# Two-layer decoder trunk on one core: the load and first norm of the first token tile, rearranged

## The chip, the cores and the metric

One core of one Trainium2 chip runs the whole kernel. The metric is device time in microseconds (us), the median of three runs. Engines named below: PE (TensorE), DVE (VectorE), ACT (ScalarE), POOL (GpSimd), SP (SyncE, which here only issues DMAs).

## What is computed

512 tokens of width 2048 pass through two layers. Each layer is `x = x + rms_norm(mixer(rms_norm(x, norm_pre)), norm_post)`.

- Layer 0: one input projection of 7168 columns (`h @ w_in`), then eight gated linear recurrence heads (HGRN2) and eight chunked gMLP groups, a concatenation and an output projection.
- Layer 1: latent attention with 16 heads (low-rank q and kv, a shared rotary key), a SiLU gate and an output projection.

What the change touches is the very first step, `rms_norm(x, norm_pre[0])`, which is `x * rsqrt(mean(x*x) + 1e-6) * w`, on its way into the first projection. All arithmetic is float32. Each float32 operand of a projection is split into a high part (rounded to the fp32r format of PE) and a low part (the rest), and a product is three matmuls: high by high, high by low, low by high.

## The kernel before

Tokens are cut into four tiles of 128. `pre_norm(i)` (L283) treats tile i: ACT squares its four chunks of 512 columns with a running sum (L286), DVE adds the four sums (L288), POOL makes the reciprocal root (`rstd_of`, L271 and L272: a multiply-add and a power), DVE scales each chunk by it and by the weight row (L292), PE transposes the chunk in four blocks against an identity (L297), ACT casts the transposed chunk into `R` as its high part (L279) and DVE subtracts to get the low part (L280). The scaled chunks lie in `B[:, 8..11]` for even tiles and `B[:, 12..15]` for odd ones. The squares themselves are not needed; their target, a junk buffer, is `G[:, 8]` for all four tiles.

The weight row `norm_pre[0]` comes by one DMA into four partitions (0, 32, 64, 96) of `B[:, 4..7]` (L97), which two engines zero first (L96). Four shuffles on DVE (L346) then spread it to all partitions.

Weights come in pieces of 512 KB. `fetch` (L147) requests one into `raw` (three buffers), `wload` (L153) splits it: ACT casts the high part `whi` (L168), DVE subtracts for the low part `wlo` (L169); `whi` and `wlo` have four buffers each. The first projection, `ia` for head pair 0, is tile-major: for token tile 0 it runs all 16 blocks of the contraction (L209 to L211, three matmuls of 256 columns each, against pieces 0 to 3), then for tile 1, and so on. ACT copies each tile's result out (L550). So tile i's matmuls need its own 16 transposed blocks, and all four tiles need pieces 0 to 3. After `ia` the projections need all four tiles at once.

All DMAs are issued by SP, in its own order. Two kinds of order matter. In the source, `at(n, f)` (L195) holds a function back until n weight pieces have been used (`tick`, L199); without it work is traced where it stands. From the traced program the Tile framework then plans the order of the instructions of each engine at compile time, by its own estimates, earlier traced work first among what it takes to be ready. At run time each engine keeps to this order and waits at the head of its queue. So an instruction traced late can stand early where the planner took the engine to be free.

The small jobs of the start: the identity (`make_identity`, L103), three small loads into `pk` (L108 to L110), which `setup_cols` (L116) transposes and uses, and `setup_masks` (L363), which builds a mask by four POOL selects (L366, L370), a DVE cast (L372) and several memsets for the recurrence heads.

Of the kernel before, what the change touches and what calls it, by code (L numbers as in the profile page):

```python
# [14 lines left out]
AF = mybir.ActivationFunctionType  # L15
ALU = mybir.AluOpType
AX = mybir.AxisListType

P = 128
# [25 lines left out]
def trunk_kernel(ctx, tc, x, positions, norm_pre, norm_post, ev_w_in, ev_lb_logits, ev_a_onorm,  # L45
                 ev_b_ln_w, ev_b_ln_b, ev_b_ws, ev_b_bias, ev_w_out, od_w_in, od_q_norm, od_w_qb,
                 od_kv_norm, od_w_kvb, od_w_out, inv_freq, out, x1_dram):
    nc = tc.nc
# [14 lines left out]
    def tp_bank():  # L63
        return ptp.tile([P, 512], F32, name="tp", tag="tp")

    R = big.tile([P, 32, 512], F32R, name="R")
    B = big.tile([P, 16, 512], F32, name="B")
    G = big.tile([P, 9, 512], F32, name="G")
    PT2 = big.tile([P, 512], F32R, name="PT2")

    def new_w(name, dt=F32):
        return big.tile([P, 16, 512], dt, name=name, tag="W")

# [12 lines left out]
    x_t = x2.rearrange("(i p) d -> i p d", p=P)  # L86
# [3 lines left out]
    def row_bc(dst, src_row):  # L90
        nc.sync.dma_start(out=dst, in_=src_row.partition_broadcast(P))

    # ---------------------------------------------------------------- constants
    W = new_w("Wa")
    for c in range(4):
        (nc.vector if c % 2 else nc.gpsimd).memset(B[:, 4 + c, :], 0.0)  # L96
    nc.sync.dma_start(out=B[0:P:32, 4:8, :],  # L97
                      in_=norm_pre[0].partition_broadcast(4).rearrange("q (c n) -> q c n", c=4))
    for c in range(4):
        nc.sync.dma_start(out=W[:, c, :], in_=x_t[0][:, c * 512:(c + 1) * 512])  # L100

    ident = const.tile([P, P], F32, name="ident")
    make_identity(nc, ident)  # L103
    mhalf = const.tile([P, 8], F32, name="mhalf")
    nc.gpsimd.memset(mhalf, -0.5)

    pk = const.tile([18, P], F32, name="pk")
    nc.sync.dma_start(out=pk[0:16, :], in_=ev_lb_logits.rearrange("l (h p) -> (l h) p", p=P))  # L108
    nc.sync.dma_start(out=pk[16:17, :], in_=ev_a_onorm)
    nc.sync.dma_start(out=pk[17:18, :], in_=inv_freq)  # L110

    cols = const.tile([P, 18], F32, name="cols")
    lb = const.tile([P, 8], F32, name="lb")
# [14 lines left out]
        nc.vector.tensor_tensor(lb, e[:, 1], e[:, 3], ALU.mult)  # L128
        nc.vector.tensor_scalar(oml, lb, -1.0, 1.0, ALU.mult, ALU.add)

    # ---------------------------------------------------------------- weights
    def wview(w):
        return w.rearrange("(k p) c -> p k c", p=P)

# [54 lines left out]
        issue_to(n + AHEAD)  # L189
        return ready.pop(n)  # L190

    # work that is traced behind a given number of weight pieces
    clock, tasks, seq = [0], [], [0]

    def at(delay, fn):  # L195
        seq[0] += 1
        tasks.append((clock[0] + delay, seq[0], fn))
# [71 lines left out]
    def rstd_of(ss, n, ncols, name, bufs=2):  # L269
        r = sm.tile([P, ncols], F32, name=name, bufs=bufs)  # L270
        nc.gpsimd.tensor_scalar(r, ss, 1.0 / n, EPS, ALU.mult, ALU.add)  # L271
        nc.gpsimd.tensor_tensor(r, r, mhalf[:, 0:ncols], ALU.pow)  # L272
        return r
# [4 lines left out]
    def split_into(dst_hi, dst_lo, src):  # L278
        nc.scalar.copy(dst_hi, src)  # L279
        nc.vector.tensor_tensor(dst_lo, src, dst_hi.bitcast(F32), ALU.subtract)  # L280

    # ------------------------------------------------------- pre norm of one token tile
    def pre_norm(i, chunks, wbc, hbuf, junk, defer=None):  # L283
        ss = sm.tile([P, 4], F32, name="pss")
        for c in range(4):
            nc.scalar.activation(junk, chunks[c], AF.Square, accum_out=ss[:, c:c + 1])  # L286
        s1 = sm.tile([P, 1], F32, name="ps1")
        nc.vector.tensor_reduce(s1, ss, AX.X, ALU.add)  # L288
        r = rstd_of(s1, D, 1, "prs", 1)

        def scale(c):
            nc.vector.scalar_tensor_tensor(hbuf[c], chunks[c], r, wbc[c], ALU.mult, ALU.mult)  # L292

        def transpose(c):
            tp = tp_bank()
            for j in range(4):
                nc.tensor.transpose(tp[:, j * P:(j + 1) * P], hbuf[c][:, j * P:(j + 1) * P], ident)  # L297
            sl = slice(i * P, (i + 1) * P)
            tpv = tp.rearrange("p (j t) -> p j t", j=4)
            split_into(R[:, 8 * c:8 * c + 8:2, sl], R[:, 8 * c + 1:8 * c + 8:2, sl], tpv)  # L300

        def step(c):
            scale(c)
            transpose(c)

        for c in range(4):
            if defer is None:
                step(c)
            else:
                at(defer + c // 2, lambda c=c: step(c))  # L310

    # ================================================================ layer 0
    ew, ow = wview(ev_w_in[0]), wview(od_w_in[0])
    qv, kvv = wview(od_w_qb[0]), wview(od_w_kvb[0])
    cuts_q = ((0, 128), (128, 192))
# [25 lines left out]
        pl["kv", p] = plan_chunk(kvv, p * 512, 512, 4, 2)  # L341
    plan_out("oo", od_w_out[0])

    wpre = [B[:, 4 + c, :] for c in range(4)]
    for c in range(4):
        nc.vector.stream_shuffle(wpre[c], wpre[c], [0] * 32)  # L346
    for i in range(NT):
        if i > 0:
            for c in range(4):
                nc.sync.dma_start(out=W[:, 4 * i + c, :], in_=x_t[i][:, c * 512:(c + 1) * 512])  # L350
            if i == 1:
                issue_to(3)
        else:
            for q in range(2):
                fetch(q)
        pre_norm(i, [W[:, 4 * i + c, :] for c in range(4)], wpre,
                 [B[:, 8 + 4 * (i % 2) + c, :] for c in range(4)], G[:, 8, :])

    mask = const.tile([P, P], U8, name="mask")
    r8 = const.tile([P, 4, 32], F32, name="r8")  # L360
# [2 lines left out]
    def setup_masks():  # L363
        mf = G[:, 7, 0:P]
        nc.gpsimd.memset(mf, 1.0)
        nc.gpsimd.affine_select(mf, mf, pattern=[[1, P]], compare_op=ALU.is_ge, fill=0.0,  # L366
                                base=0, channel_multiplier=-1)
        for b in range(1, 4):
            blk = mf[:, b * 32:(b + 1) * 32]
            nc.gpsimd.affine_select(blk, blk, pattern=[[0, 32]], compare_op=ALU.is_ge, fill=0.0,  # L370
                                    base=-32 * b, channel_multiplier=1)
        nc.vector.tensor_copy(mask, mf)  # L372
        nc.vector.memset(r8, 0.0)
        nc.vector.memset(r8[:, 0, 0::8], 1.0)
        nc.vector.memset(r8[:, 1, 7::8], 1.0)
        nc.vector.memset(r8[:, 2, 0::4], 1.0)
        nc.vector.memset(r8[:, 3, 3::4], 1.0)
        nc.vector.memset(pw, 1.0)
        nc.gpsimd.memset(G[:, 8, :], 0.0)

    setup_masks()
    S_sb = new_hs("S_sb", F32)
    nc.gpsimd.memset(S_sb, 0.0)

    cosT = const.tile([P, T], F32, name="cosT")
    sinT = const.tile([P, T], F32, name="sinT")
# [20 lines left out]
        nc.scalar.activation(sinT, r, AF.Sin, scale=sgn[:, 0:1])  # L407
        nc.scalar.activation(cosT, n, AF.Sin, scale=-1.0, bias=sgn[:, 1:2])

    # ------------------------------------------------------- HGRN2 of one head  # L410
    def t4(a):
        return a.rearrange("p (b t) -> p b t", b=4)

    def hgrn_vec(h):
        par = h % 2
        f, sg, q = W[:, par, :], W[:, 2 + par, :], W[:, 4 + par, :]
        A, kdg, KK1, kD = W[:, 8, :], W[:, 9, :], W[:, 10, :], W[:, 11, :]
        k128, q128 = W[:, 12, :], W[:, 13, :]
# [151 lines left out]
        hgrn_head(2 * p + 1, 5)  # L570
        proj_feat(pl["ga", p], r_act, ga_evac)

    # ------------------------------------------------------- gMLP, two groups at a time
    for p in range(4):
        vg = W[:, 0:2, :].rearrange("p g (i c) -> p g i c", i=4)
        lnw = B[:, 14, :].rearrange("p (w c) -> p w c", w=2)
# [57 lines left out]
        proj_feat(pl["ub", p], r_act, ub_evac)  # L634
        proj_feat(pl["gb", p], r_act, gb_evac)

    # ------------------------------------------------------- output projection, post norm, residual
    def out_proj(Wy, name, wpost_row, resid_t, junk, finish, early=KD, hook=None):
        def split_cat(k0, k1):
            for k in range(k0, k1):  # L640
# [56 lines left out]

    out_proj(W, "eo", norm_post[0], x_t, G[:, 8, :], finish0)

    # ================================================================ layer 1  # L700
    row_bc(B[:, 0, :], od_q_norm[0])
    row_bc(B[:, 1, :], od_kv_norm[0])
    C = low_rank_act()
# [39 lines left out]
        nc.gpsimd.tensor_tensor(sw[0:n], sw[0:n], sinT[0:n], ALU.mult)  # L743
        nc.vector.tensor_tensor(dst[0:n], dst[0:n], sw[0:n], ALU.add)

    # shared rotary key
    kps = mm_bank()
    stk, _ = piece(pl["kpe"])
    for k in range(KD):
# [14 lines left out]

    low_rank("ckv", B[:, 1, :], [G[:, 4 + i, :] for i in range(4)], 8, False)

    # gate path
    for c in range(8):
        def gate_evac(m, ps, c=c):
            g = B[:, 2 * c + m, :]  # L770
# [189 lines left out]
```

## Time and profile before

| what | value |
|---|---|
| median of three runs | 1623.61 us (1623.47 to 1623.64) |
| profiled execution, span on the core | 1621.9 us |
| median less span (what lies around the span) | 1.7 us |
| PE busy in the span | 1588.8 us (98%) |
| DVE, ACT, POOL busy | 760.4, 536.8, 100.8 us |
| first PE instruction | 11.05 us after the span's start |

No time of the profiled execution is given apart from its span, so its own time is taken as the span and the 1.7 us around it. The page shows PE busy from the second fortieth of the span to the last; a fortieth is 40.5 us. A busy PE is not a PE at its peak: 128x256 matmuls that start 0.12 us apart are shown with 0.28 us each.

### The profile page before, as it was taken

To read this page: it belongs to the slowest core of one execution; us is meant where nothing else is said; L and a number is where in the kernel's file an instruction comes from. 1 tells how busy PE (TensorE), PEld (TensorE's weight loads), DVE (VectorE), ACT (ScalarE), POOL (GpSimd) and SP (SyncE) were. 2 spreads that over 40 slices of the span, in tenths; PEclk is the share of its full clock that TensorE was granted. 3 is DMA by queue.
4 is the path that set the end of the run, shared out by engine and by line. 5 is a ranking of instruction groups with operands and counts; after the bars stand their busy time and mean duration, and the time that the engine had idled before them with its cause. 6 is when DMAs were issued, how large, how long until landed. Compare 5 with 4: busy or idle time off the path is not lost.

```text
span 1621.9 us, 22372 instructions
## 1 busy us (share of the span) xinstructions
PE 1588.8 (98%) x9185; PEld 1397.2 (86%) x9185; DVE 760.4 (47%) x1351; ACT 536.8 (33%) x938; POOL 100.8 (6%) x163
## 2 busy tenths in 40 slices
PE   6999999999999999999999999999999999999997
PEld 5889898898989898888899999888888888888887
DVE  7653544535534343453226543232266667663234
ACT  6322222222222212232225432222255565552221
POOL 1000000000120120200001000000000000000000
PEclk9999999999999999999999999999999999999999
DMA  6422322323233333343336423333221121232324
GB/s 205 121 85 79 92 88 77 94 81 96 89 117 98 101 85 111 115 136 100 105 97 189 137 65 92 104 92 100 85 66 56 59 59 58 93 104 92 104 91 156
DMA packets 133394, 161.14 MB, mean 99 GB/s; under 512 B 7958, under 2 KB 104744, under 8 KB 133288
## 3 DMA queue, kind: packets, MB, share of 16 engines
q1 hardware_dynamic: 133292, 159.71, 32.1%
q8 instruction: 72, 1.18, 0.3%
q14 instruction: 30, 0.25, 0.1%
HBM read 151.30 MB, written 8.39 MB: 98 GB/s over the span
## 4 chain that ended last, share of the span: by engine, by line
PE 90%; DVE 5%; ACT 2%; POOL 1%; issue 1%; DMA 1%; DVEq 0%; POOLq 0%; SPq 0%; ACTq 0%
PE mm L214 14%; PE mm L216 14%; PE mm L215 14%; PE mm L211 13%; PE mm L210 13%; PE mm L209 13%; DVE R L280 2%; PE sc L485 1%; PE sc L890 1%; DVE wlo L169 1%; DVE sc L864 1%; ACT G L868 1%; PE tp L297 1%; PE sc L891 1%; DVE R L820 1%
## 5 line engine op out<-in xcount | busy, mean ns | idle before, releaser
L169 DVE TENSOR_TENSOR wlo<-raw,whi 128x1024 fp32r<-128x1024 f32 x240 | 300.1, 1251 | 614.5 <-ACT whi L168 597.6
L168 ACT CAST whi<-raw 128x1024 fp32r<-128x1024 f32 x240 | 252.2, 1052 | 767.7 <-PE mm L215 353.0
L209 PE MATMUL mm<-whi,R 128*128 128x256 f32 (+1 forms) x1408 | 442.0, 314 | 0.1
L210 PE MATMUL mm<-wlo,R 128*128 128x256 f32 (+1 forms) x1408 | 440.6, 313 | 1.2 <-DVE wlo L169 1.2
L211 PE MATMUL mm<-whi,R 128*128 128x256 f32 (+1 forms) x1408 | 440.5, 313 | 0.0
L214 PE MATMUL mm<-R,whi 128*128 128x512 f32 x896 | 351.4, 392 | 0.0
L216 PE MATMUL mm<-R,wlo 128*128 128x512 f32 x896 | 348.9, 389 | 0.0
L215 PE MATMUL mm<-R,whi 128*128 128x512 f32 x896 | 348.8, 389 | 0.0
L210 PEld LDWEIGHTS mm<-wlo,R 128*128 128x128 f32 x1408 | 268.8, 191 | 16.8 <-DVE wlo L169 1.7
L209 PEld LDWEIGHTS mm<-whi,R 128*128 128x128 f32 x1408 | 268.8, 191 | 15.4 <-ACT whi L168 0.3
L211 PEld LDWEIGHTS mm<-whi,R 128*128 128x128 f32 x1408 | 268.8, 191 | 15.0
L216 PEld LDWEIGHTS mm<-R,wlo 128*128 128x128 f32 x896 | 168.2, 188 | 35.2
L214 PEld LDWEIGHTS mm<-R,whi 128*128 128x128 f32 x896 | 168.3, 188 | 34.5
L215 PEld LDWEIGHTS mm<-R,whi 128*128 128x128 f32 x896 | 168.3, 188 | 34.2
L214 PE MATMUL mm<-Wc,whi 128*128 128x512 f32 x160 | 62.8, 393 | 0.0
L215 PE MATMUL mm<-Wc,whi 128*128 128x512 f32 x160 | 62.7, 392 | 0.0
L216 PE MATMUL mm<-Wc,wlo 128*128 128x512 f32 x160 | 62.5, 390 | 0.0
L280 DVE TENSOR_TENSOR R<-mm,R 128x512 fp32r<-128x512 f32 x48 | 33.1, 689 | 31.3 <-ACT R L279 31.1
L280 DVE TENSOR_TENSOR R<-tp,R 128x512 fp32r<-128x512 f32 x64 | 42.7, 686 | 2.5 <-ACT R L279 1.9
L279 ACT CAST R<-tp 128x512 fp32r<-128x512 f32 x64 | 36.1, 592 | 17.6 <-PE tp L297 16.5
L279 ACT CAST R<-mm 128x512 fp32r<-128x512 f32 x48 | 28.1, 586 | 38.0 <-PE mm L216 19.5
L868 ACT ACTIVATE G<-sc,nm 128x512 f32<-128x512 f32 (+2 forms) x48 | 26.1, 545 | 35.2 <-DVE nm L867 35.1
(237 smaller groups left out, 1552.7 us busy)
## 6 DMA issues: line engine op xcount, KB each, us to landing
raw<-in_ev_w_in_dram SPq DMA_DIRECT2D x112, 512.0 KB, 3.6
raw<-in_od_w_in_dram SPq DMA_DIRECT2D x49, 512.0 KB, 3.9
raw<-in_ev_w_out_dram SPq DMA_DIRECT2D x32, 512.0 KB, 3.6
raw<-in_od_w_out_dram SPq DMA_DIRECT2D x32, 512.0 KB, 3.6
raw<-in_od_w_kvb_dram SPq DMA_DIRECT2D x16, 512.0 KB, 3.7
raw<-in_od_w_qb_dram SPq DMA_DIRECT2D x16, 384.0 KB, 3.3
Wa<-in_x_dram SPq DMA_DIRECT2D x16, 256.0 KB, 5.6
G<-in_x_dram SPq DMA_DIRECT2D x16, 256.0 KB, 4.8
```

The costliest lines, as they stand in the source:

```text
L168: nc.scalar.copy(hi[:, 0:n], raw[:, 0:n])
L169: nc.vector.tensor_tensor(lo[:, 0:n], raw[:, 0:n], hi[:, 0:n].bitcast(F32), ALU.subtract)
L209: nc.tensor.matmul(o, hh[:, sl], wh, start=first, stop=False, skip_group_check=True)
L210: nc.tensor.matmul(o, hh[:, sl], wl, start=False, stop=False, skip_group_check=True)
L211: nc.tensor.matmul(o, hl[:, sl], wh, start=False, stop=last, skip_group_check=True)
L214: nc.tensor.matmul(ps, hi, hh, start=first, stop=False)
L215: nc.tensor.matmul(ps, hi, hl, start=False, stop=False)
L216: nc.tensor.matmul(ps, lo, hh, start=False, stop=last)
L279: nc.scalar.copy(dst_hi, src)
L280: nc.vector.tensor_tensor(dst_lo, src, dst_hi.bitcast(F32), ALU.subtract)
L297: nc.tensor.transpose(tp[:, j * P:(j + 1) * P], hbuf[c][:, j * P:(j + 1) * P], ident)
L868: nc.scalar.activation(pv[j], sp[j], AF.Exp, bias=nm[:, j:j + 1], scale=C_SCALE, accum_out=su[:, j:j + 1])
```

## The change

Seven edits:

1. The four chunks of token tile 0 are requested first of all, chunks 0 and 2 on SP, chunks 1 and 3 on ACT's queue. Before, SP issued all four, and the request for the norm row stood between them.
2. For tile 0, DVE squares chunks 1 and 3 (`tensor_tensor_reduce` into `G[:, 5]`), ACT chunks 0 and 2.
3. For tile 1, the junk target of the squares is `B[:, 11]`, which holds the scaled chunk 3 of tile 0 until it has been transposed.
4. The three small loads into `pk` are issued after all loads of x.
5. `setup_masks` and the memset of `S_sb` are held back by one weight piece.
6. 24 transposes of the identity by itself run on PE, traced ahead of the shuffles; nothing reads their results.
7. Comment lines go.

```diff
     W = new_w("Wa")
+    for c in range(4):
+        (nc.sync if c % 2 == 0 else nc.scalar).dma_start(out=W[:, c, :], in_=x_t[0][:, c * 512:(c + 1) * 512])
     for c in range(4):
         (nc.vector if c % 2 else nc.gpsimd).memset(B[:, 4 + c, :], 0.0)
     nc.sync.dma_start(out=B[0:P:32, 4:8, :],
                       in_=norm_pre[0].partition_broadcast(4).rearrange("q (c n) -> q c n", c=4))
-    for c in range(4):
-        nc.sync.dma_start(out=W[:, c, :], in_=x_t[0][:, c * 512:(c + 1) * 512])
-
     ident = const.tile([P, P], F32, name="ident")
...
-    nc.sync.dma_start(out=pk[0:16, :], in_=ev_lb_logits.rearrange("l (h p) -> (l h) p", p=P))
-    nc.sync.dma_start(out=pk[16:17, :], in_=ev_a_onorm)
-    nc.sync.dma_start(out=pk[17:18, :], in_=inv_freq)
...
+    def pre_norm(i, chunks, wbc, hbuf, junk, defer=None, junk2=None):
         ss = sm.tile([P, 4], F32, name="pss")
         for c in range(4):
-            nc.scalar.activation(junk, chunks[c], AF.Square, accum_out=ss[:, c:c + 1])
+            if junk2 is not None and c % 2:
+                nc.vector.tensor_tensor_reduce(out=junk2, in0=chunks[c], in1=chunks[c], scale=1.0, scalar=0.0,
+                                               op0=ALU.mult, op1=ALU.add, accum_out=ss[:, c:c + 1])
+            else:
+                nc.scalar.activation(junk, chunks[c], AF.Square, accum_out=ss[:, c:c + 1])
...
+    for _ in range(3):
+        warm = tp_bank()
+        for j in range(8):
+            nc.tensor.transpose(warm[:, (j % 4) * P:(j % 4 + 1) * P], ident, ident)
     wpre = [B[:, 4 + c, :] for c in range(4)]
...
-                 [B[:, 8 + 4 * (i % 2) + c, :] for c in range(4)], G[:, 8, :])
+                 [B[:, 8 + 4 * (i % 2) + c, :] for c in range(4)], B[:, 11, :] if i == 1 else G[:, 8, :],
+                 junk2=G[:, 5, :] if i == 0 else None)
+
+    nc.sync.dma_start(out=pk[0:16, :], in_=ev_lb_logits.rearrange("l (h p) -> (l h) p", p=P))
+    nc.sync.dma_start(out=pk[16:17, :], in_=ev_a_onorm)
+    nc.sync.dma_start(out=pk[17:18, :], in_=inv_freq)
...
-    setup_masks()
+    at(1, setup_masks)
     S_sb = new_hs("S_sb", F32)
-    nc.gpsimd.memset(S_sb, 0.0)
+    at(1, lambda: nc.gpsimd.memset(S_sb, 0.0))
```

## Rows read from the trace of the kernel before

**Rows 1.** The line of the page that gives each engine's busy time, share of the span and count of instructions.

```profile
PE 1588.8 (98%) x9185; PEld 1397.2 (86%) x9185; DVE 760.4 (47%) x1351; ACT 536.8 (33%) x938; POOL 100.8 (6%) x163
```

**Rows 2.** Busy time by stretch: from and to in us, length, busy us of each engine with the count of its instructions, PE clock granted, share and rate (GB/s) of DMA.

```profile
0.00:50.00 50.00, 35.75 (x260) 33.52 (x261) 38.42 (x81) 30.96 (x63) 7.42 (x25) 1.00 0.57 179
50.00:400.00 350.00, 350.00 (x2009) 306.22 (x2008) 169.18 (x244) 93.86 (x140) 20.94 (x40) 1.00 0.29 90
...
37.85:50.50 12.65, 12.65 (x100) 12.27 (x101) 10.83 (x24) 7.12 (x11) 0.44 (x1) 1.00 0.27 73
20.39:41.11 20.72, 18.41 (x149) 17.36 (x149) 18.61 (x31) 13.27 (x32) 2.02 (x5) 1.00 0.48 158
```

**Rows 3.** The chain that ended last, five of its pieces in the first 16 us: start, length, what.

```profile
2.08 3.90 DMA B<-in_norm_pre_dram
6.13 2.62 DVE B L346 x4
9.13 0.55 POOL G L370 x3
...
14.17 0.58 PE mm L210
14.77 1.12 PE tp L297 x4
```

**Rows 4.** SP's queue in order of time: start, length over which the merged requests were issued, line, target and source, count.

```profile
0.79 0.86 SPq L100 DMA_DIRECT2D Wa<-in_x_dram  x2
2.08 0.66 SPq L97 DMA_DIRECT2D B<-in_norm_pre_dram  x1
2.80 0.86 SPq L100 DMA_DIRECT2D Wa<-in_x_dram  x2
...
4.80 0.95 SPq L150 DMA_DIRECT2D raw<-in_ev_w_in_dram  x2
```

**Rows 5.** Busy time by stretch, columns as in rows 2: two stretches while the first loads are under way.

```profile
2.00:4.00 2.00, 0.00 (x0) 0.00 (x0) 0.70 (x11) 0.08 (x2) 1.55 (x4) 1.00 0.86 243
4.00:6.00 2.00, 0.00 (x0) 0.00 (x0) 0.00 (x0) 1.43 (x4) 0.00 (x0) 1.00 0.76 188
```

**Rows 6.** Instructions of DVE, ACT and POOL for token tile 0 in order of time: start, length, engine, line, what, shape; in brackets the idle time before it and what ended it.

```profile
2.41 0.35 DVE L404 MEMSET sgn<- 32x1 f32 x4
...
3.99 0.63 ACT L286 ACTIVATE G<-Wa 128x512 f32<-128x512 f32 x1 [1.92 <-DMA Wa<-in_x_dram]
...
7.00 0.63 ACT L286 ACTIVATE G<-Wa 128x512 f32<-128x512 f32 x1 [1.50 <-DMA Wa<-in_x_dram]
...
8.63 0.14 DVE L288 TENSOR_REDUCE ps<-pss 128x1 f32<-128x4 f32 x1
8.87 0.19 POOL L271 TENSOR_SCALAR prs<-ps 128x1 f32<-128x1 f32 x1 [5.28 <-DVE ps L288]
...
10.24 2.74 DVE L292 SCALAR_TENSOR_TENSOR B<-Wa,prs,B 128x512 f32<-128x512 f32 x4 [0.30 <-POOL prs L272]
```

**Rows 7.** The same instruction (`tensor_tensor_reduce`) where layer 1 uses it, by line and shape: count, busy us, mean ns of one, idle before.

```profile
L864 DVE CUSTOM_DVE_ANT_0 sc<-sc,G 128x512 f32<-128x512 f32 x16 | 11.0, 690 | 0.0
```

**Rows 8.** PE in order of time, columns as in rows 6: four rows of tile 0 and one of tile 2; and the busy time of the stretch just behind PE's last instruction, columns as in rows 2.

```profile
11.05 1.97 PE L297 MATMUL tp<-ident,B 128*128 128x128 f32 x8 [11.05 <-DVE B L292]
...
16.11 1.05 PE L297 MATMUL tp<-ident,B 128*128 128x128 f32 x4
...
17.82 0.41 PE L211 MATMUL mm<-whi,R 128*128 128x256 f32 x1
...
18.19 0.28 PE L210 MATMUL mm<-wlo,R 128*128 128x256 f32 x1
...
30.74 0.60 PE L297 MATMUL tp<-ident,B 128*128 128x128 f32 x4
...
1614.00:1616.00 2.00, 0.00 (x0) 0.00 (x0) 0.89 (x3) 0.13 (x2) 0.74 (x2) 0.89 0.81 310
```

**Rows 9.** ACT, DVE, POOL and PE (PEld is its weight load) around token tile 1 in order of time, columns as in rows 6, and the first reader of `pk`.

```profile
17.21 0.59 ACT L279 CAST R<-tp 128x512 fp32r<-128x512 f32 x1
17.69 0.63 ACT L286 ACTIVATE G<-Wa 128x512 f32<-128x512 f32 x1
18.44 0.63 ACT L286 ACTIVATE G<-Wa 128x512 f32<-128x512 f32 x1
19.07 1.98 ACT L168 CAST whi<-raw 128x1024 fp32r<-128x1024 f32 x2
19.20 0.16 DVE L288 TENSOR_REDUCE ps<-pss 128x1 f32<-128x4 f32 x1 [0.68 <-ACT G L286]
19.52 0.19 POOL L271 TENSOR_SCALAR prs<-ps 128x1 f32<-128x1 f32 x1 [9.32 <-DVE ps L288]
20.16 0.19 PEld L209 LDWEIGHTS mm<-whi,R 128*128 128x128 f32 x1 [0.33 <-ACT whi L168]
20.39 0.75 DVE L292 SCALAR_TENSOR_TENSOR B<-Wa,prs,B 128x512 f32<-128x512 f32 x1 [1.03 <-POOL prs L272]
21.06 1.22 DVE L169 TENSOR_TENSOR wlo<-raw,whi 128x1024 fp32r<-128x1024 f32 x1
22.33 0.39 PE L210 MATMUL mm<-wlo,R 128*128 128x256 f32 x1 [0.41 <-DVE wlo L169]
39.93 0.23 PE L118 MATMUL tp<-ident,pk 18*128 18x18 f32 x1
```

More of the change, by code (lines that the diff above doesn't have):

```diff
@@ L280, in split_into @@
         nc.vector.tensor_tensor(dst_lo, src, dst_hi.bitcast(F32), ALU.subtract)
-    def pre_norm(i, chunks, wbc, hbuf, junk, defer=None):
+    def pre_norm(i, chunks, wbc, hbuf, junk, defer=None, junk2=None):
         ss = sm.tile([P, 4], F32, name="pss")
         for c in range(4):
-            nc.scalar.activation(junk, chunks[c], AF.Square, accum_out=ss[:, c:c + 1])
+            if junk2 is not None and c % 2:
[3 more added lines that the diff above has]
+                nc.scalar.activation(junk, chunks[c], AF.Square, accum_out=ss[:, c:c + 1])
         s1 = sm.tile([P, 1], F32, name="ps1")
```

## The prediction

> **What bounds the kernel now.** I read the page's line of engines first. PE is busy 98% of the span [rows 1], so the reader should ask only where PE is not busy or not at its pace. Busy time by stretch answers it: in the first 50 us PE is busy for 35.75, in the next 350 for all 350 [rows 2]. The change lies wholly in those first 50 us. There I read the chain of waits, then each engine in order of time.
>
> To 10.24 us the chain runs over the norm row: its DMA (requested at 2.08, landed 3.9 us later), four shuffles on DVE (6.13, 2.62 us together), then POOL, where three mask selects (0.55 us) stand ahead of the power [rows 3]. Beside it runs a second path just as long: the four chunks of x, the last two of which ACT got at 7.00 and after [rows 6]; the sum on DVE starts at 8.63, when shuffles and squares are both over. The first scale starts at 10.24 and PE's first transpose at 11.05 [rows 6, 8].
>
> From there to about 20 us four engines wait for each other in turn. From 20.39 to 41.11 DVE is the limit: 18.61 of 20.72 us busy, by scales, splits and the low parts of two weight pieces. Then PE has work in hand: 12.65 of 12.65 us from 37.85 to 50.50 [rows 2]. So a gain counts if it brings forward tile 1's first scale at 20.39, takes work out of DVE's stretch behind it, or fills PE's waits.
>
> The sum is made against the profiled execution: a span of 1621.9 us with 1.7 around it, 1623.6 in all, which is the median shown.
>
> **The change part by part.**
>
> *First scale of tile 0.* SP's two requests of chunks took 0.86 us and so do ACT's two, before anything else it has to do; ACT got its first chunk at 3.99 after 1.92 us idle [rows 4, 6], which hides the 0.86. Chunks 2 and 3 are asked for some 1.6 us earlier (about 1.2 in place of 2.80). But the norm row, which cannot be asked for before the memsets are over (2.08), now stands behind chunk 2 as well, while the DMA engines were already 86% and 76% busy [rows 4, 5]. At 243 GB/s half a megabyte is 2.1 us, so the row lands 0 to 2.1 us later. Two squares come to DVE at 0.69 each [rows 7]; they cost nothing if done before the row is in. Best case: row at 6.1, sum taken ahead of the shuffles, scale right behind them at 8.75, that is 1.5 earlier. Worst: shuffles end at 10.85, and sum, POOL and the rest of the way (8.63 to 10.24, 1.61) come behind them: 12.5, 2.2 later. Nothing in the rows is near either end, so I take the middle, +0.3.
>
> *Mask work.* From POOL's first step to the scale it is 1.37 us for tile 0 (8.87 to 10.24) and 0.87 for tile 1 (19.52 to 20.39) [rows 6, 9]; the selects are the difference, 0.5. But a memset due only at the twelfth weight piece (L404) ran at 2.41 [rows 6]: the planner fills idle engines early whatever the trace order, so the selects may stay. 0 to -0.5; I take the middle, -0.25. The DVE memsets that are held back too stood in idle time before 3 us, and none is needed within 50 us.
>
> *Warm-up.* 24 transposes at 1.97/8 = 0.25 us [rows 8] are 5.9 us on an idle PE; the identity is ready at about 2.4, so they end by 8.4, ahead of the first real one even at 8.75 plus 0.8. The granted clock is listed as 1.00 there [rows 2], yet transposes of tile 0 take 1.05 to 1.12 us in fours against 0.60 later, and matmuls 0.41 up to 17.82 against 0.28 from 18.19 [rows 3, 8]: PE ran at the lower level (1.2 GHz) until about 18 and at 2.4 GHz then. Between the first scale and the end of tile 0's transposes (17.16) the chain holds one matmul (0.58 against 0.28) and two such fours: 0.30 + 0.52 + 0.45 = 1.3 us. If PE enters at the upper level, 1.3 is saved; if not, 0. Against it: in the stretch from 1614 to 1616, where PE has no instruction left, the grant averages 0.89, so it falls there [rows 8]; and the warm-up would stop 1 us or more (up to 4.9 with the late first scale) before the real work. I take half, -0.65. The page "TensorE: Matmul & The Clock Gate" of the Trainium skill says (Part 4: PE-mode transpose) that transposes do not count as PE activity for the clock as matmuls do. By that rule this term is 0 and the sum below 0.65 higher; no row decides it, since transposes and matmuls are mixed in the low stretch.
>
> *Tile 1's squares.* With the junk in `B[:, 11]` all four wait until PE has transposed tile 0's last chunk (17.16 before); two of them used to run ahead of that. Behind each wait in ACT's queue stand the squares of tile 2 and any cast planned later. Before, the sum followed 2.04 us after 17.16 (19.20). Now it needs a cast (0.48, 17.21 to 17.69) and four squares at 0.75 (17.69 to 18.44): 3.6 with the hand-over [rows 9], 1.5 later. Lower end 0, if the squares no longer break up the casts; upper end is the rival below. I take +1.5.
>
> *What fills that wait.* The casts of pieces 2 and 3 stood behind the squares (19.07 to 21.05), and their low parts (1.2 each, 21.06 and later) in DVE's limiting stretch [rows 9]. With ACT waiting, the planner can move them ahead: 0 to -2.4. Piece 3 is asked for late (its buffer waits for piece 0), so I take one piece, -1.2. PE's own waits for piece 2 (0.33 at 20.16 and 0.41 at 22.33) then go: -0.75.
>
> *No cost.* The three `pk` loads leave SP's queue ahead of the weights (at 4.80) and pass twelve loads of x; their reader runs at 39.93 [rows 4, 9], far behind. Weight requests move up, at most to 2.74 where the norm row's request ends, but DMA is nearly full and DVE's scales end at 12.98, so the first low part could not start sooner. If the plan put that reader ahead of the loads' landing, PE would stall with all it holds behind it.
>
> Sum: +0.3 - 0.25 - 0.65 + 1.5 - 1.2 - 0.75 = -1.05. Prediction 1622.6.
>
> **Rivals.**
>
> *The start opens fully.* Row early (-1.5), clock up (-1.3), squares as above (+1.5), both pieces ahead (-2.4), PE's waits gone (-0.75): -4.4 or 1619.2. For it: each end is possible by the rows. Against: it needs the norm row to pass 1 MB of x.
>
> *Slower: ACT stands behind piece 3.* The planner puts the cast of piece 3 ahead of tile 1's squares, since it is traced earlier, and on the chip ACT waits for that load with the squares behind it. Before, the second cast ran to 21.05. Then squares 3.0 and sum to scale 1.19 (19.20 to 20.39) bring tile 1's first scale to 25.2 in place of 20.39; less two low parts already done, 2.4, that is +2.4: 1626.0. It decides from a cast that starts at 17.6 or later (17.6 + 1.0 + 3.0 + 1.2 - 2.4 = 20.4). For it: the trace order. Against: piece 0 is split earlier, so piece 3 may be there.
>
> *The warm-up does nothing and the selects stay.* The clock is low until tile 0's matmuls have run, whatever ran before: 0.65 and 0.25 drop out of the sum: 1623.5. The Trainium skill's rule on transposes, named above, would give this.
>
> **How the numbers follow.** The forecast 0.45 (its own range 1621.2 to 1624.0), the open start 0.22, the slower case 0.18, no effect of the warm-up 0.15. All low ends together give -1.5 - 0.5 - 1.3 - 2.4 - 0.75 = -6.4 with the squares at 0; all high ends 2.2 + 2.4 = +4.6; one in ten at each side is left out: 1618.7 to 1625.9. This kernel's measurement tells 0.2%, 3.25 us, from no change. Faster than that (under 1620.4) is most of the open start and a little of the forecast, 0.24; slower (over 1626.9) is the slower case with a late first scale on top, 0.08; 0.68 lies within.
>
> **What would show it.** First scale between 8.75 and 12.5: the norm row's landing and the place of the sum among the shuffles tell which. Transposes of tile 0 at 0.6 us a four: the warm-up held; at 1.05: it did not. Squares of tile 1 all behind tile 0's last transposes, and the casts of pieces 2 and 3 before or behind them. DVE's last split of tile 3 (41.1 before) and the end of `ia` (about 50.5 before) should move by about -1. The prediction is wrong if PE's later stretch moves: a new wait behind 50 us, or a plan that shifted there.

## The result, and the profile after

| | us |
|---|---|
| before, median of 20 runs | 1623.62 (1623.24 to 1624.03) |
| after, median of 20 runs | 1626.58 (1625.72 to 1627.39) |
| ratio | 1.0017, 95% interval [1.0011, 1.0023] |
| span of the profiled execution, before and after | 1621.9, 1624.3 |

The change makes the kernel 3.0 us slower. 1622.6 was predicted, with a range up to 1625.9. The 3.0 us are below the 0.2% (3.25 us) up to which the prediction speaks of no change, but they are clear of noise (the interval leaves out 1), outside the range and on the other side of the forecast.

The same views as ahead of the prediction, of the kernel after. In its file L286 and L283 are the squares on ACT and DVE, L288 the sum, L267 and L268 the root on POOL, L292 the scale, L297 the transposes, L275 and L276 the high and low part of a transposed chunk, L164 and L165 those of a weight piece, L351 the shuffles, L376 and L380 the selects, L382 the mask cast, L348 the warm-up, L560 the copy of `ia`. The page's line of engines, to be held against [rows 1]:

```profile
PE 1593.1 (98%) x9209; PEld 1401.4 (86%) x9209; DVE 761.5 (47%) x1355; ACT 535.0 (33%) x934; POOL 100.6 (6%) x163
```

PE has 24 instructions and 4.3 us more, which is the warm-up. Busy time by stretch, columns as in [rows 2]:

```profile
8.00:10.00 2.00, 0.00 (x0) 0.00 (x0) 2.00 (x7) 1.05 (x2) 1.98 (x5) 0.70 1.04 354
10.00:18.00 8.00, 4.96 (x20) 4.18 (x21) 7.90 (x12) 3.85 (x5) 0.24 (x2) 0.50 0.81 270
24.85:43.86 19.01, 16.04 (x126) 14.70 (x127) 16.24 (x29) 10.14 (x24) 2.04 (x5) 1.00 0.29 84
...
50.00:400.00 350.00, 350.00 (x2017) 306.65 (x2016) 169.74 (x244) 96.29 (x142) 20.88 (x40) 1.00 0.29 90
```

Behind 50 us nothing changed: PE is busy for all 350 us, as before, and its last matmul starts at 1615.85 in place of 1613.28, 2.57 later, about as much as at the end of `ia` (below). The loss was made in the first 50. The third row is DVE's limiting stretch, from tile 1's first scale to tile 3's last split (the low part of a transposed chunk): 19.01 us in place of 20.72 [rows 2], but begun at 24.85 in place of 20.39. The first two show the clock: granted at 0.70 in the mean from 8 to 10 us, at 0.50 (the lower level, 1.2 GHz) to 18.

Token tile 0 in order of time, DVE and POOL, columns as in [rows 6]:

```profile
4.73 0.69 DVE L283 CUSTOM_DVE_ANT_0 G<-Wa 128x512 f32<-128x512 f32 x1 [1.86 <-DMA Wa<-in_x_dram]
6.71 0.69 DVE L283 CUSTOM_DVE_ANT_0 G<-Wa 128x512 f32<-128x512 f32 x1 [1.28 <-DMA Wa<-in_x_dram]
7.51 0.16 DVE L288 TENSOR_REDUCE ps<-pss 128x1 f32<-128x4 f32 x1
7.66 0.73 DVE L351 STREAM_SHUFFLE B<-B 128x512 f32<-128x512 f32 x1
8.02 0.29 POOL L376 TENSOR_SCALAR_AFFINE_SELECT G<-G 128x128 f32<-128x128 f32 x1
8.28 0.55 POOL L268 TENSOR_TENSOR prs<-prs,mhalf 128x1 f32<-128x1 f32 x1
10.19 2.72 DVE L292 SCALAR_TENSOR_TENSOR B<-Wa,prs,B 128x512 f32<-128x512 f32 x4
```

The sum is 1.1 us earlier than in [rows 6] and the root is ready at 8.8, but the first scale moved from 10.24 to 10.19 only: the four shuffles now stand behind DVE's two squares and end at 10.2. The first shuffle (7.66) shows no wait for the norm row, so the row was there by then.

PE in order of time, to be held against [rows 8]:

```profile
2.49 4.24 PE L348 MATMUL tp<-ident 128*128 128x128 f32 x24 [2.49 <-POOL ident masks.py:199]
11.07 1.94 PE L297 MATMUL tp<-ident,B 128*128 128x128 f32 x8 [4.34 <-DVE B L292]
...
15.98 1.12 PE L297 MATMUL tp<-ident,B 128*128 128x128 f32 x4 [1.29 <-DVE R L276]
...
17.32 1.06 PE L297 MATMUL tp<-ident,B 128*128 128x128 f32 x4
```

The warm-up ended at 6.73, not near 8.4 as predicted: the 24 took 4.24 us, 0.18 each. 4.34 us of idle time lie between it and the first real transposes, and these take what they took before: 1.94, 1.12, 1.06. New is the wait of 1.29 for a low part on DVE: tile 0's last transposes end at 18.38 in place of 17.16.

DVE, ACT and POOL around token tile 1, to be held against [rows 9]:

```profile
12.83 2.35 DVE L165 TENSOR_TENSOR wlo<-raw,whi 128x1024 fp32r<-128x1024 f32 x2
15.23 1.28 DVE L276 TENSOR_TENSOR R<-tp,R 128x512 fp32r<-128x512 f32 x2
14.18 1.05 ACT L164 CAST whi<-raw 128x1024 fp32r<-128x1024 f32 x1 [0.55 <-DMA raw<-in_ev_w_in_dram]
...
18.41 0.59 ACT L275 CAST R<-tp 128x512 fp32r<-128x512 f32 x1 [0.69 <-PE tp L297]
18.89 0.64 ACT L286 ACTIVATE B<-Wa 128x512 f32<-128x512 f32 x1
19.52 1.03 ACT L164 CAST whi<-raw 128x1024 fp32r<-128x1024 f32 x1
20.45 0.63 ACT L286 ACTIVATE B<-Wa 128x512 f32<-128x512 f32 x1
21.08 0.62 ACT L286 ACTIVATE G<-Wa 128x512 f32<-128x512 f32 x1
21.69 0.62 ACT L286 ACTIVATE B<-Wa 128x512 f32<-128x512 f32 x1
22.31 0.62 ACT L286 ACTIVATE G<-Wa 128x512 f32<-128x512 f32 x1
22.92 0.62 ACT L286 ACTIVATE B<-Wa 128x512 f32<-128x512 f32 x1
23.66 0.16 DVE L288 TENSOR_REDUCE ps<-pss 128x1 f32<-128x4 f32 x1 [1.85 <-ACT B L286]
24.85 2.74 DVE L292 SCALAR_TENSOR_TENSOR B<-Wa,prs,B 128x512 f32<-128x512 f32 x4 [1.04 <-POOL prs L268]
...
43.17 0.69 DVE L276 TENSOR_TENSOR R<-tp,R 128x512 fp32r<-128x512 f32 x1 [0.58 <-ACT R L275]
53.31 0.35 ACT L560 COPY G<-mm 128x256 f32<-128x256 f32 x1
```

The target tells the squares apart: `B` is tile 1, `G` is tile 2. Tile 1's four squares begin at 18.89, once their junk target is free (18.38) and tile 0's last cast is done, and are spread to 23.54, with the cast of piece 3 and two squares of tile 2 in between. The sum comes at 23.66 (19.20 before), the first scale at 24.85 (+4.46). The shorter stretch behind it gives 1.71 back: DVE's last split is at 43.17 (40.42 before), the last copy of `ia` at 53.31 (50.70), the span 2.4 longer.

### The profile page after: what moved, and what is told of

Read it like the earlier page. It is cut to its first block, busy times and chain, and to the rows that moved or that the text cites. A ratio compares the mean times of both kernels' runs of the same rounds, so it can differ in the third digit from the quotient of the medians.

```text
span 1624.3 us, 22413 instructions
## 1 busy us (share of the span) xinstructions
PE 1593.1 (98%) x9209; PEld 1401.4 (86%) x9209; DVE 761.5 (47%) x1355; ACT 535.0 (33%) x934; POOL 100.6 (6%) x163
## 4 chain that ended last, share of the span: by engine, by line
PE 90%; DVE 5%; ACT 2%; issue 1%; POOL 1%; DMA 0%; DVEq 0%; ACTq 0%; POOLq 0%
PE mm L210 14%; PE mm L212 14%; PE mm L211 14%; PE mm L205 13%; PE mm L207 13%; PE mm L206 13%; DVE R L276 2%; PE sc L495 1%; PE sc L900 1%; PE tp L297 1%; DVE sc L874 1%; ACT G L878 1%; DVE wlo L165 1%; PE sc L901 1%; DVE R L830 1%
## 5 line engine op out<-in xcount | busy, mean ns | idle before, releaser
L165 DVE TENSOR_TENSOR wlo<-raw,whi 128x1024 fp32r<-128x1024 f32 x240 | 299.9, 1250 | 615.0 <-ACT whi L164 594.7
L164 ACT CAST whi<-raw 128x1024 fp32r<-128x1024 f32 x240 | 252.1, 1051 | 768.1 <-PE mm L211 355.6
L276 DVE TENSOR_TENSOR R<-mm,R 128x512 fp32r<-128x512 f32 x48 | 33.1, 689 | 31.4 <-ACT R L275 31.2
L276 DVE TENSOR_TENSOR R<-tp,R 128x512 fp32r<-128x512 f32 x64 | 42.6, 685 | 2.6 <-ACT R L275 2.1
L275 ACT CAST R<-tp 128x512 fp32r<-128x512 f32 x64 | 36.1, 592 | 21.5 <-PE tp L297 20.4
L275 ACT CAST R<-mm 128x512 fp32r<-128x512 f32 x48 | 28.1, 586 | 38.1 <-PE mm L212 19.5
```

Of the source, the lines that this page charges most:

```text
L164: nc.scalar.copy(hi[:, 0:n], raw[:, 0:n])
L165: nc.vector.tensor_tensor(lo[:, 0:n], raw[:, 0:n], hi[:, 0:n].bitcast(F32), ALU.subtract)
```

## The experiments

Each run was timed beside the kernel before on the same chip; "against before" is the difference of the two medians. The interval of each ratio reaches some 1.5 us to each side, so smaller differences are read from the traces. Three rows of each trace serve as a yardstick: the first scale of tile 1, DVE's last split of tile 3 and the last copy of `ia`. But a trace is one execution. Tile 0's first scale, ahead of which edit 3 changes nothing and edit 6 only adds work on an idle PE, starts at 10.24 (before), 9.63 (3 alone) and 10.46 (6 alone), so under 0.8 us a row counts only against an earlier row of its own trace. The span scatters too: from PE's last matmul to its end the traces take 8.1 to 9.2 us.

| edits present | against before | first scale, tile 1 | last split | last copy of `ia` | span |
|---|---|---|---|---|---|
| none | 0 | 20.39 | 40.42 | 50.70 | 1621.9 |
| all | +3.0 | 24.85 | 43.17 | 53.31 | 1624.3 |
| all but 3 | -1.4 | 16.44 | 38.38 | 49.12 | 1620.3 |
| 3 alone | +0.5 | 22.62 | 41.72 | 51.98 | 1622.9 |
| all but 6 | +1.9 | 24.19 | 42.33 | 52.60 | 1623.5 |
| 6 alone | +0.4 | 22.44 | 40.47 | 50.74 | 1622.6 |
| all but 3 and 6 | -1.0 | 21.30 | 40.16 | 50.18 | 1621.1 |

### Edit 3, the junk target

Undone in the kernel after:

```diff
-                 [B[:, 8 + 4 * (i % 2) + c, :] for c in range(4)], B[:, 11, :] if i == 1 else G[:, 8, :],
+                 [B[:, 8 + 4 * (i % 2) + c, :] for c in range(4)], G[:, 8, :],
```

> The changed kernel with edit 3 undone: tile 1's squares go to G[:, 8] again. Theory (hold): the 3.0 us lost come from tile 1's squares, which the junk in B[:, 11] holds behind tile 0's last transposes, so that tile 1's first scale starts at 24.85 instead of 20.39; without it the scale starts at 21 or before and the time falls by 2 to 3 us, to 1623.6 to 1624.6. Rival (order on DVE): the loss is tile 0's own, because two low parts of weights and the mask cast (2.4 us) stand ahead of its first low part on DVE; then undoing edit 3 gives back under 1 us, 1625.6 or more. A third way: the freed squares are planned ahead of tile 0's casts on ACT and hold those up until tile 1's chunks land; then tile 0's last transposes end later than 18.4 us.

Measured: 1622.02 against 1623.40 before, ratio 0.9992 [0.9983, 1.0001]. DVE and ACT around tile 1:

```profile
10.93 0.62 ACT L286 ACTIVATE G<-Wa 128x512 f32<-128x512 f32 x1
15.04 0.14 DVE L288 TENSOR_REDUCE ps<-pss 128x1 f32<-128x4 f32 x1
16.44 0.73 DVE L292 SCALAR_TENSOR_TENSOR B<-Wa,prs,B 128x512 f32<-128x512 f32 x1
```

Without the hold the planner puts tile 1's squares into ACT's idle time from 10.93 on, ahead of tile 0's first cast. In the medians the change gains 1.4 without this edit; the edit takes 4.3.

Put alone into the kernel before (same line, the other way):

> The kernel before with edit 3 alone: only the junk target of tile 1's squares is moved to B[:, 11]. Theory (hold): tile 1's squares all run behind tile 0's last transposes, its first scale moves from 20.39 to 22.5 to 23.5 us, one low part leaves the stretch behind it, and the time rises by 1 to 2 us to 1624.6 to 1625.6. Rival (order on DVE): no change beyond 0.5 us, 1623.6.

Measured: 1623.92 against 1623.40, ratio 1.0003 [0.9995, 1.0012]. There the squares start at 17.10, and three of them stand in one piece. So the edit's price is no constant: in the old order 0.5 in the medians, inside the interval (1.3 at the last copy of `ia` in the trace, which is that of the slowest of the eleven executions), in the new one 4.3.

Is it the hold, or only the other buffer? Tile 1's squares write into a piece of the same buffer that nothing holds:

```diff
-                 ..., B[:, 11, :] if i == 1 else G[:, 8, :],
+                 ..., B[:, 15, :] if i == 1 else G[:, 8, :],
```

> The changed kernel, where the junk target of tile 1 is another piece of the same buffer, the one that nothing holds at that time (tile 1's own fourth scaled chunk), so the squares are moved out of the common junk buffer but held by nothing. Theory: edit 3 costs what it costs because of the hold alone, so this equals the run with edit 3 undone: 1622.0, tile 1's four squares from 10.9 on, tile 1's first scale at 16.4. Rival: moving the target out of the common junk buffer costs something by itself (that buffer also carries the mask build and a memset on POOL): between 1622.0 and 1626.6.

Measured: 1622.13 against 1623.68, ratio 0.9992 [0.9983, 1.0001]: the time and the order of the run with edit 3 undone. It is the hold.

And tile 2's squares in between? They get the same held target, so the planner has no reason to take them first:

```diff
-                 ..., B[:, 11, :] if i == 1 else G[:, 8, :],
+                 ..., B[:, 11, :] if i in (1, 2) else G[:, 8, :],
```

> The changed kernel with tile 2's squares on the same held junk target as tile 1's, so that the planner no longer mixes them in between tile 1's: one square of tile 1, piece 3's cast, then the other three squares of tile 1 in one piece. Theory: of the 4.5 us by which tile 1's first scale is late, the squares of tile 2 in between account for about 1.3 (two of 0.63), the cast of piece 3 for 1.0 and the hold itself for the rest: sum near 22.4, first scale near 23.6, time 1625.4. Rival: the mixing costs nothing, since tile 2's squares have to be done anyway and DVE waits for them next: 1626.6.

Measured: 1625.38 against 1623.68, +1.7 in place of +3.0. DVE at tile 1:

```profile
22.45 0.16 DVE L288 TENSOR_REDUCE ps<-pss 128x1 f32<-128x4 f32 x1 [0.91 <-ACT B L286]
23.64 2.74 DVE L292 SCALAR_TENSOR_TENSOR B<-Wa,prs,B 128x512 f32<-128x512 f32 x4 [1.03 <-POOL prs L268]
```

The sum is 1.21 earlier, and so is the first scale. Of this 0.27 was there before: the first square starts at 18.62 in place of 18.89. From it to the sum are 3.83 us in place of 4.77, 0.94 less; the two squares of tile 2 had taken 1.22, but tile 1's now start 0.75 apart where they follow each other, not 0.62. The medians differ by 1.3.

### Edit 6, the warm-up

Taken out of the kernel after (the four lines of the 24 transposes):

> The changed kernel without the 24 transposes of the identity. If the warm-up has no effect on the clock of tile 0's work (the clock rose during it and fell again before 11 us), the time of the instructions of tile 0 is the same, 1.05 to 1.12 us for four transposes, and the total stays within 0.5 us of 1626.6, but for what a different plan brings. If the warm-up matters, the total rises by 1 us or more. Order on DVE: with the first low part of tile 0 planned ahead of the weights' low parts, tile 0's last transposes end 1 us earlier than 18.4 and the total falls by up to 1 us.

Measured: 1625.26 against 1623.40, ratio 1.0012 [1.0003, 1.0020]; 1.1 less than with it in the medians, 0.7 to 0.8 in the traces from the last copy of `ia` on. DVE and PE at tile 0:

```profile
12.73 0.67 DVE L276 TENSOR_TENSOR R<-tp,R 128x512 fp32r<-128x512 f32 x1
...
16.04 1.06 PE L297 MATMUL tp<-ident,B 128*128 128x128 f32 x4
```

Fours of transposes take 1.12 and 1.06 as before, so the warm-up had brought no clock. What goes is an order: without the 24 transposes tile 0's first low part (12.73) stands ahead of the weight's, presumably because the planner takes PE to be free earlier; the last transposes end at 17.10 in place of 18.38. Only half of that reaches tile 1's first scale (24.19 in place of 24.85), because three squares of tile 2 now stand among tile 1's, not two.

Alone, in the kernel before:

> The kernel before with edit 6 alone (24 identity transposes). Theory: the clock falls again between the end of the warm-up (near 6.7 us) and the first real transposes (near 11), so nothing is gained; the planner counts the warm-up as PE time and puts both low parts of pieces 0 and 1 ahead of tile 0's first low part, which costs about 1.2 us of PE wait: 1624.8, fours of transposes still 1.05 to 1.12 us. Rival: the clock that the warm-up raises is worth something even so (one of the two fours of transposes at 0.6): 1622.5 to 1623.6.

Measured: 1624.10 against 1623.75, ratio 1.0002 [0.9993, 1.001]. Both the lost order (PE waits 1.16 us for tile 0's low part at 16.12) and the fours at 1.11 and 1.05 are there, but not its price of 1.2: 0.4 in the medians, 0.04 at the last copy of `ia`. Tile 1's first scale is 2.05 later, but one weight low part (20.12) stands ahead of it that stood behind it before, and DVE's last split is at 40.47 (40.42 before).

Longer, 56 transposes (`range(3)` to `range(7)`), so that it reaches up to the real ones:

> The changed kernel with 56 instead of 24 transposes of the identity, so that PE works until just ahead of the first real transposes at 11.07 us. If only the idle gap from 6.73 to 11.07 undid the warm-up, the granted clock stays at the upper level, tile 0's fours of transposes take 0.6 us, and its last transposes end about 1 us earlier than 18.4; the total falls by 0.5 to 1.5 us to 1625.1 to 1626.1. If transposes cannot hold the clock, the fours stay at 1.05 and the total at 1626.6. If tile 1's hold hides it, the fours are short and the total falls by less than 0.5.

Measured: 1629.89 against 1623.40, ratio 1.0040 [1.0027, 1.0053]. The transposes of the warm-up by source line, in the kernel after and in this run (count, duration in ns min/median/max, first and last start in us):

```profile
L348 PE MATMUL tp<-ident x24: 272/420/476, 2.5 to 6.5; 128*128 128x128 f32 x24
```

```profile
L348 PE MATMUL tp<-ident x56: 272/273/473, 2.5 to 10.7; 128*128 128x128 f32 x56
```

PE in order of time behind it:

```profile
10.93 1.29 PE L297 MATMUL tp<-ident,B 128*128 128x128 f32 x8
...
19.64 0.58 PE L205 MATMUL mm<-whi,R 128*128 128x256 f32 x1 [7.42 <-ACT R L275]
```

Both ends of the mechanism are here. The clock rose during the warm-up (from 0.47 us a transpose to 0.27) and held: eight real transposes take 1.29 in place of 1.94. And the planner, with still more PE time ahead, put the casts of pieces 2 and 3 ahead of tile 0's first casts; ACT waited for piece 3's load, and PE 7.42 us for ACT. In that wait the clock fell: the fours behind it take 1.12 and 1.06 again.

The clock without that side effect: edit 3 undone, and the 24 transposes take x's fourth chunk as input, so they start when it lands. At the start the order on DVE and ACT is that of the run with edit 3 undone:

```diff
-            nc.tensor.transpose(warm[:, (j % 4) * P:(j % 4 + 1) * P], ident, ident)
+            nc.tensor.transpose(warm[:, (j % 4) * P:(j % 4 + 1) * P], W[:, 3, (j % 4) * P:(j % 4 + 1) * P], ident)
```

> The changed kernel with edit 3 undone, and the 24 warm-up transposes take blocks of x's fourth chunk as input in place of the identity, so that they cannot start before that chunk has landed (6.3 to 6.7 us) and end near 10.8, just ahead of the first real transposes near 11. The order on DVE, ACT and PE at the start is that of the run with edit 3 alone undone (1622.0). Theory: the clock is then still at its upper level when the real work begins; eight transposes take 1.3 in place of 1.9, fours 0.6 in place of 1.1, and tile 0's last transposes end about 1 us earlier: 1621.0. Rival: the gain is swallowed by the casts on ACT and low parts on DVE, which set PE's pace there: 1622.0, though the transposes are faster. Third: the warm-up runs past 11 and pushes the real ones: 1622.5 or more.

Measured: 1622.01 against 1623.75, ratio 0.9989 [0.998, 0.9998]. PE in order of time, and the last copy of `ia`:

```profile
6.62 5.07 PE L348 MATMUL tp<-ident,Wa 128*128 128x128 f32 x24 [6.62 <-DMA Wa<-in_x_dram]
11.53 1.04 PE L297 MATMUL tp<-ident,B 128*128 128x128 f32 x8
...
16.00 0.66 PE L297 MATMUL tp<-ident,B 128*128 128x128 f32 x4 [1.20 <-DVE R L276]
...
47.90 0.35 ACT L560 COPY G<-mm 128x256 f32<-128x256 f32 x1
```

In this trace the clock held through to tile 1, although the warm-up ran 0.5 too long. Against the run with edit 3 undone the last copy of `ia` is 1.22 earlier, and the kernel's last group of scales is still 1.20 earlier (DVE, 1612.82 in place of 1614.02); the span is only 0.5 shorter because 0.7 more passes behind them, in the part that scatters. The trace is not typical: it lists a mean granted clock of 0.999, three other executions 0.998, and seven 0.996 or 0.997, which no execution of the kernel before has (0.998 or 0.999); in those seven the clock must have fallen for a while. The medians of the two runs (-1.7 and -1.4 against before) cannot be told apart.

With 16 transposes in place of 24:

> The run with the late warm-up (24 transposes of x's fourth chunk, edit 3 undone), with 16 transposes in place of 24. In that run the warm-up ended at 11.5 and pushed tile 0's first transposes from 11.0 to 11.5. Theory: 16 end near 10.3, the real ones start at 11.0 with the clock still at its upper level, and the whole start is 0.5 us earlier: 1621.5. Rival: the idle time between 10.3 and 11.0, or that between tile 0's first eight transposes and the first matmul, now lets the clock fall, fours of transposes take 1.1 again: 1622.0 to 1622.5. The shorter warm-up also lets the planner put tile 0's first two casts on ACT ahead of tile 1's fourth square, which should bring PE's first matmul from 14.3 to about 13.5.

Measured: 1623.20 against 1623.43, ratio 1.0 [0.9991, 1.0009]: the rival, and worse than it. PE and one stretch:

```profile
10.95 1.29 PE L297 MATMUL tp<-ident,B 128*128 128x128 f32 x8 [0.97 <-DVE B L292]
...
15.72 1.11 PE L297 MATMUL tp<-ident,B 128*128 128x128 f32 x4 [1.14 <-DVE R L276]
```

```profile
12.00:14.00 2.00, 0.46 (x4) 0.22 (x3) 2.00 (x4) 1.97 (x6) 0.00 (x0) 0.76 0.98 333
```

The first eight found the upper level, then PE idled for 1.54 us and the grant fell: 0.76 in the mean from 12 to 14 us, 0.50 in the next stretch. Here too the plan changed with eight transposes fewer: tile 0's first two casts stand ahead of tile 1's fourth square, so tile 1's sum runs at 16.16 (15.07 with 24), its first scale at 17.36 (16.47) and the last copy of `ia` at 49.91 (47.90). How much of this is the plan and how much the clock the two traces don't tell.

### Edits 3 and 6 undone, and edit 5

> The changed kernel with edit 3 (junk target of tile 1) and edit 6 (warm-up) both undone. Theory: the two losses are separate, one in the order of tile 1's squares (undone alone: -4.6 us against the changed kernel) and one in the order of the low parts that the warm-up moved (undone alone: -1.3). Both undone: 1626.6 - 4.6 - 1.3 = 1620.7, some 2.7 faster than before; tile 0's last transposes end near 17.1, its first low part runs ahead of the second weight low part. Rival: the loss is one and the same delay seen twice, because with the squares out of the way DVE's first low parts have slack: 1622, as with the squares undone alone.

Measured: 1622.71 against 1623.75, ratio 0.9994 [0.9985, 1.0003]. The two do not add up: the rival's 1622 came nearer than 1620.7, but for a cause of its own. DVE and POOL at tile 1:

```profile
19.04 0.15 DVE L288 TENSOR_REDUCE ps<-pss 128x1 f32<-128x4 f32 x1
...
19.34 1.23 DVE L165 TENSOR_TENSOR wlo<-raw,whi 128x1024 fp32r<-128x1024 f32 x1
19.35 1.26 POOL L267 TENSOR_SCALAR prs<-ps 128x1 f32<-128x1 f32 x1 [9.22 <-DVE mask L378]
...
21.30 0.75 DVE L292 SCALAR_TENSOR_TENSOR B<-Wa,prs,B 128x512 f32<-128x512 f32 x1 [0.73 <-POOL prs L268]
```

Tile 1's squares were done before 15, but in this plan its sum stands behind tile 0's last low part, at 19.04 in place of 15.04, and the first scale at 21.30 in place of 16.44. So with edit 3 undone the warm-up's plan is the better one, with edit 3 the worse.

The same with edit 5 undone as well (`setup_masks` and the memset of `S_sb` traced where they stood):

> The changed kernel with edits 3, 5 and 6 undone (what is left is the two queues for x, two squares on DVE, and the small loads behind x). DVE's, ACT's and PE's order at the start is the one of the run with edits 3 and 6 undone. Theory: holding the mask work back changed nothing, as the planner puts it in the same places, so the time is that of the other run within 0.5 us, near 1620.7, and POOL still has the selects between its two steps of the root. Rival: the held-back memsets and selects free POOL at the start, so this run is 0.3 to 0.5 slower than the other.

Measured: 1622.73 against 1623.75, ratio 0.9994 [0.9985, 1.0003]. The select stands between POOL's two steps either way (at 7.81 here). In this setting edit 5 does nothing that shows; edits 1, 2 and 4 together are worth the -1.0, whose interval includes no change (none of them was tried alone).

### A version with the order set by hand

Edits 1, 4 and 5 stay, 2 and 3 go, and the places that the planner had changed are pinned (`issue_after` queues what a block traces behind an instruction of its engine):

```diff
+        if i == 0:
+            with tc.issue_after(red.ins):
+                for c in (2, 3):
+                    nc.vector.stream_shuffle(wbc[c], wbc[c], [0] * 32)
...
+                with tc.issue_after(last_scale[0]):
+                    issue_to(1)
...
+        if i == 1:
+            with tc.issue_after(sum1[0]):
+                issue_to(3)
...
+        with tc.issue_after(last_scale[0]):
+            nc.vector.tensor_copy(mask, mf)
...
+            nc.tensor.transpose(warm[:, (j % 4) * P:(j % 4 + 1) * P], W[:, 1, (j % 4) * P:(j % 4 + 1) * P], ident)
```

> A version with the order set by hand: edits 1, 4 and 5 stay; edit 3 is undone; edit 2 is undone (ACT squares all four chunks); two shuffles stand ahead of tile 0's sum and two behind it; the low parts of pieces 0 and 1 and the mask cast stand behind tile 0's scales, those of pieces 2 and 3 behind tile 1's sum; the 24 warm-up transposes take x's second chunk as input (landed 4.7), so they end near 9.5. Theory: DVE is the limit from the first scale to tile 3's last split, so what counts is when it can start: first scale 9.2 in place of 10.2, clock at its upper level, tile 1's first scale near 15.5, last split near 36.2: 1621.0, against 1622.0 for the run with the late warm-up. Rival: the gain of the start is lost behind, where the weights behind the first projection are not ready sooner: 1622.0.

Measured: 1621.62 against 1623.68, ratio 0.9985 [0.9976, 0.9994]: 2.1 faster than before and 5.0 better against before than the change. DVE and PE:

```profile
6.89 0.01 DVE L361 LOAD_MASK_SELECT B<-B  x1 [4.03 <-DMA B<-in_norm_pre_dram]
...
9.55 2.72 DVE L300 SCALAR_TENSOR_TENSOR B<-Wa,prs,B 128x512 f32<-128x512 f32 x4
```

```profile
10.44 1.29 PE L307 MATMUL tp<-ident,B 128*128 128x128 f32 x8 [0.23 <-DVE B L300]
...
15.53 1.12 PE L307 MATMUL tp<-ident,B 128*128 128x128 f32 x4 [0.30 <-DVE R L276]
```

The first scale did come earlier, at 9.55 (9.2 expected). It could not come sooner: the first shuffle waited for the norm row until 6.89, so with the requests of edit 1 the row lands later than before, where the shuffles had it at 6.09 (5.42 and 6.29 in the traces with 3 alone and 6 alone). Behind the first eight transposes PE idled for 2.71 us and its clock fell before the next four. DVE's last two splits run from 37.63 to 39.0, not to 36.9, so the rest of the expected gain stayed out. The eleven executions spread from 1620.04 to 1622.27: the five with a mean granted clock of 0.996, the traced one among them, took 1621.6 to 1622.3, the six with 0.997 took 1620.0 to 1621.7. No trace shows what the clock did in those six.

## Why the prediction was wrong, step by step

- **Tile 1's squares: the step that failed.** This term of the sum was taken as +1.5, with one rival above it; the first scale came 4.46 later. The working was: a cast (0.48), then four squares in one piece (3.0), from 17.16. The rows after give from 18.38: cast 0.51, four squares 2.49, two squares of tile 2 1.22, the cast of piece 3 0.93, hand-over 0.13, together 5.28; and the start itself 1.22 later than 17.16. The prediction did name the squares of tile 2 and a cast, but as standing behind tile 1's squares: what counts is what the planner puts in between once these are no longer ready first. Undoing the edit gives 4.3 back in the medians, keeping tile 2's squares out 1.3 (0.94 of it seen in the trace between the first square and the sum). The 1.22 of the start is the warm-up's order (17.10 without it).
- **First scale: +0.3 taken, -0.05 measured**, which is less than traces of the same path differ by. The size came out near by luck, since two things cancel. Gained: the sum is ahead of the shuffles, as in the best case, so the scale follows them at once, not 1.5 later. Lost: the shuffles begin at 7.66 in place of 6.13. By the version ordered by hand some 0.8 of that is the row itself, inside the predicted 0 to 2.1; the other 0.7 are DVE's own square of chunk 3, which ran at 6.71, and the sum. "They cost nothing if done before the row is in" was the right question, and the answer was no.
- **Mask work: -0.25 taken, 0 measured.** The doubt beside it (the planner fills idle engines whatever the trace order) was the answer; and the root was ready at 8.8, long before the shuffles ended, so the scale did not wait for it.
- **Warm-up: -0.65 taken, nothing gained in clock, 1.1 lost in order** (0.7 to 0.8 by the traces). Half a gain was taken for a gap of 1 to 4.9 us; it was 4.34 and the clock fell in it. That 24 unread transposes could cost anything through the plan was not thought of.
- **What fills the wait: -1.2 taken, -1.7 measured.** Both pieces' low parts left DVE's stretch, as the far bound had it. PE's waits (-0.75) were no term of their own: the path there runs over DVE.
- **The rival "ACT stands behind piece 3"** said 25.2 for the first scale and 1626.0; 24.85 and 1626.6 came. Its price came near, in part by luck, for its mechanism was half right: the cast does stand among the squares, at 19.52 (behind the 17.6 from which it was to decide), but ACT did not wait for the load and the cast itself takes 0.93. Tile 2's squares and the warm-up's order did the rest. It had 0.18.
- **The Trainium skill's rule** on transposes ("TensorE: Matmul & The Clock Gate", Part 4: PE-mode transpose) would have put the warm-up's gain in clock at 0, which is what came, but not for its reason. The transposes did raise the clock here: 273 ns in the median over 56 of them, from 473 at most, and 1.29 for the eight behind. The gain was lost in the idle time behind the warm-up.

## What to carry to other kernels

Where a planner sets the order, an edit that makes work wait also decides what is put ahead of it: ask for the order of that engine after the edit, not only for the wait. Work that "costs nothing" on an idle engine still costs planned time, and can reorder the others. A warm-up of TensorE shortened the first real transposes (1.04 to 1.29 for eight in place of 1.94) only in the four traces where it ended within 1 us of them, and in three of these the clock fell again in PE's next wait (1.54, 2.71 and 7.42 us). No run shows a gain in time from it that is clear of noise.

## Of the hardware, not expected

- TensorE's clock after a warm-up. In the kernel after, PE was busy from 2.49 to 6.73 and then idle; the grant averaged 0.70 from 8 to 10 us and 0.50 from there to 18. With the same 24 transposes it was still 1.00 up to 10 and averaged 0.58 from 10 to 11 in the run with edit 3 undone, and it was 1.00 up to 11 and averaged 0.51 from 11 to 12 in the run with edit 6 alone: the moment of the fall moves by some 2 us from trace to trace. In the trace with 24 late transposes the grant stayed at 1.00 over an idle time of 1.73 us; in the one with 16 it fell in one of 1.54, in the version ordered by hand (24) in one of 2.71. With such scatter one trace each does not tell whether the number of transposes mattered.
- POOL slows down beside DVE. The one-column step L267 takes 0.19 us in most rows and 1.26 beside a weight's low part of 1.23 (the run without edits 3 and 6). Beside tile 0's low parts, of whose two inputs one is in PSUM, it took 0.19 (the run with edit 3 undone, 15.34). In the version ordered by hand three selects that take 0.55 elsewhere took 4.26, beside scales and low parts:

```profile
10.36 4.26 POOL L394 TENSOR_SCALAR_AFFINE_SELECT G<-G 128x32 f32<-128x32 f32 x3
```

The page "GPSIMD Engine Reference" of the Trainium skill (1. Specifications) says that POOL shares its SBUF interfaces with VectorE and meets contention from DVE instructions with two SBUF inputs. The trace agrees: the low part reads `raw` and `whi`, and the step ended when it did (20.61 and 20.57). No run here took the DVE instruction away.
